# More warming products, new due times for the head, and a new order of the attention steps in a hybrid decoder layer

## The chip, the cores and the metric

One core of one Trainium2 chip runs the whole layer. The metric is the device time of one execution in microseconds (us). Engine names: PE is TensorE (matrix products and transposes), DVE is VectorE, ACT is ScalarE, POOL is GpSimd, SP is SyncE, which here issues the DMAs.

## The reference

A sequence of 512 tokens with width 1024, one layer:

```python
ada = silu(c) @ w_ada + b_ada;  shift, scale, gate = split(ada, 3)
h = rms_norm(x) * (1 + scale) + shift
z = h @ w_in               # 3072 columns: xl | gl | q | k | v | ga, 512 each
y_lru = rg_lru(conv4(xl)) * silu(gl)
q, k = rms_norm per head (8 heads of 64)
y_att = moba_attention(q, k, v) * silu(ga)   # blocks of 256: own block causal, past block whole
out = x + gate * (concat(y_lru, y_att) @ w_out)
```

With 512 tokens there are two blocks, so the attention is ordinary causal attention over tiles of 128 queries.

## The kernel before, in words

All large products are made in three terms (high by high, low by high, high by low parts in float32r), each 512 columns wide. The stages follow one another on PE. In the head, x is loaded in four tiles of 128 tokens (t), its rows are normalised (ACT squares and sums, POOL takes the power, DVE scales, line 423), and eight groups of four transposes (`x_tr(t, i)`: token tile t, half i of the width, line 398) bring it into `xs[i]`, by way of PSUM banks 0, 1, 6 and 7, each used twice. `cb` is silu(c) broadcast to all partitions by two small groups of products (line 380). With it DVE forms two columns of the adaLN product for each slice k of the width (`dot`, line 460); from these come `gs` and the first `h` slices (lines 478 to 492). Then layer 1 (`mm1`, line 509) runs k = 0 to 7 for eight accumulators, `xl0` to `xl3` in banks 4 to 7 and `gl0` to `gl3` in banks 0 to 3. It is followed by k, q and v, the tiles of the attention gate (`g_tile`, line 878), the attention, and the output units (`unit`, line 854).

Warming products (line 442) are 128x128 bf16 products of zeros, two to a group. Their result is read by nobody. The groups have a chain among them, since they write one bank, and they must precede the accumulator that uses their bank next.

Nothing runs in the order of the code. `Plan.schedule` puts all operations in one order by list scheduling with estimated costs: an operation has a due time (`dl`), given or worked back from its successors, and a release time (`rel`). In each turn it takes the engine that can start first, and of that engine's ready operations that could start within 0.35 us of it (0.2 us after the planned time T0 = 14.5) the one with the smallest start plus weighted due time (weight 1.0 before T0, 0.1 after). PE products without a due time of their own take the running sum of PE's costs, so the order of the program is their due order. On the chip each engine runs its own list strictly in this order and waits by semaphores.

The attention is written as steps in `ORDER`: `S` scores of one head pair (hp) for query tiles a and a+1 (a = 2 or 0), then a softmax on DVE, ACT and POOL; `T` transposes of P; `P` the products P.T V; `F` one tile of the attention gate (`F3` in bank 3, else in bank 0); `G` the broadcast of the residual gate, in bank 3; `W` the outputs of the recurrence and the pieces of w_out; `U` the output units of tiles 3 and 2. Joined steps (`P00+P01`) are one visit. The products P.T V of one a and two neighbouring hp share a tile in bank 3:

```python
if hp % 2 == 0:
    pv[a] = bank(f"pv{a}{hp}", 3)
    yy[a] = slot(f"y{a}{hp}")
```

Of the kernel before, what the change touches and what calls it, by code (L numbers as in the profile page):

```python
# [17 lines left out]
P = 128  # L18
S = 512
D = 1024  # L20
# [9 lines left out]

NSLOT = 69
RESERVE = 10
ORDER = ("F3 S22 F S20 S21 T22 G F T21 F3 T20 P20 S23 S01 S02 S00 T00 P21 T23 S03 W T01 P22 T03 T02 P00+P01 "
         "P02 P23 P03 U")
TURN = 0.05
AHEAD = 200.0
SAME, SWITCH = 0.13, 0.2
EPS_PICK, ALPHA = 0.2, 0.1
NDV = 3
DL = dict(cs=60.2, cr=70.1, cbp=18.7, cbc=8.5, rb=47.8, ad=12.3, gs=44.2)  # L40
CBP = 9.0
NSTAGE = 3
NC1 = 1024
T0, TK, LEAD, NWARM, WSTEP, DIP = 14.5, 5.45, 4.0, 36, 0.175, 0.8
RAW, EPS0, ALPHA0, LATER = 4, 0.35, 1.0, 15.5


# [21 lines left out]
class Plan:  # L69
# [13 lines left out]
    def bank(self, name, i):  # L83
        b = Buf(name, "bank", bank=i)
        b.prev = self.banks.get(i)
        self.banks[i] = b
        return b
# [7 lines left out]
    def op(self, fn, costs, reads=(), writes=(), out_lat=None, dl=None, rel=0.0, window=None, sbuf=None, bulk=False, bias=None, mode="full"):  # L95
        o = Op(len(self.ops), fn, costs, out_lat)
        o.mode = mode
        o.bulk, o.bias = bulk, self.bias if bias is None else bias
        o.est, o.sbuf, o.free = rel, True, window
        for lst, wr in ((reads, False), (writes, True)):  # L100
            for x in lst:
                b, key = x if isinstance(x, tuple) else (x, None)
                if b.prev is not None:
                    o.preds.update(b.prev.ops)
                for k2, (ws, rs) in b.state.items():
                    if key is None or k2 is None or key == k2:
                        o.preds.update(ws)
                        if wr:
                            o.preds.update(rs)
                if wr:  # L110
                    if key is None:
                        b.state = {}
                    b.state[key] = ([o], [])
                else:
                    b.state.setdefault(key, ([], []))[1].append(o)
                if not b.ops or b.ops[-1] is not o:
                    b.ops.append(o)
                o.bufs.append(b)
                if b.kind == "bank":
                    o.sbuf = False  # L120
        if sbuf is not None:
            o.sbuf = sbuf
        o.preds.discard(o)
        for p in o.preds:
            p.succs.append(o)
        o.own = "PE" in costs and dl is None
        if "PE" in costs:
            o.dl = o.want = self.pe_t
            self.pe_t += costs["PE"]
        if dl is not None:  # L130
            o.dl = dl
        self.ops.append(o)
        return o
# [111 lines left out]
def hybrid_layer_kernel(ctx: ExitStack, tc, x, small, bgate, wbd, wad, w1, wp, out):  # L245
# [4 lines left out]
    ps = ctx.enter_context(tc.tile_pool(name="ps", bufs=1, space=bass.MemoryType.PSUM))  # L250
    pl = Plan(13.0, 26.0, 40.0, {"DVE": 0.5})
    op, slot, bank, wide = pl.op, pl.slot, pl.bank, pl.wide

    def fixed(name, shape, dt=F32):
        return Buf(name, "fixed", t=cp.tile(shape, dt, name=name))


    def copy(dst, d_ap, src, s_ap, n, psum=False, scale=None, reads=(), bulk=False, bias=None):

        ap = 0 if scale is None else 1  # L260

        def fn(e):
            if e is act:
                act.activation(d_ap(), s_ap(), AF.Copy, scale=1.0 if scale is None else scale())  # L264
            elif scale is None:
                dve.tensor_copy(d_ap(), s_ap())
            else:
                dve.tensor_scalar(d_ap(), s_ap(), scale(), None, op0=MULT)
        return op(fn, {"ACT": c_act(n, ap, psum), "DVE": c_dve(n, ap, psum, not psum)}, [src, *reads], [dst],
                  bulk=bulk, bias=bias)  # L270

    def tt(dst, d_ap, a, a_ap, b, b_ap, n, alu, psum=False, dve_only=False, rel=0.0, window=None):
        def fn(e):
            e.tensor_tensor(d_ap(), a_ap(), b_ap(), op=alu)  # L274
        costs = {"DVE": c_dve(n)} if psum or dve_only else c_tt(n)
        return op(fn, costs, [a, b], [dst], rel=rel, window=window)
# [27 lines left out]
    warm, nhalf = fixed("warm", [P, 128], BF16), fixed("nhalf", [P, 8])  # L304
# [16 lines left out]
    def col(base, i=0, n=1):  # L321
        return sm.t[:, base + i:base + i + n]

    cs, hb, gqk = fixed("cs", [P, 8]), fixed("hb", [P, 8]), fixed("gqk", [P, 1])
    gm, ga_ = fixed("gm", [P, 8, 2]), fixed("gad", [P, 8, 2])
    op(lambda e: act.activation(cs.t, col(C_C, 0, 8), AF.Tanh, scale=0.5), {"ACT": 0.2}, [sm], [cs], dl=DL["cs"])

# [41 lines left out]
    tiny(lambda: dve.tensor_scalar(sp4.t, sp4.t, 4.0, None, op0=MULT), [], [sp4])  # L369


    cr, cb, cbp = fixed("cr", [8, P]), fixed("cb", [P, D]), [bank("cb0", 3), bank("cb1", 5)]
    c8 = sm.t[0:8, C_ROW:C_ROW + P]
    op(lambda e: act.activation(cr.t, c8, AF.Tanh, scale=0.5), {"ACT": 0.22}, [sm], [cr], dl=DL["cr"])
    op(lambda e: dve.scalar_tensor_tensor(cr.t, cr.t, 1.0, c8, op0=ADD, op1=MULT), {"DVE": 0.24}, [sm], [cr], sbuf=False)
    for i in range(2):
        def mm_c(e, i=i):
            for j in range(4):
                d = 4 * i + j
                pe.matmul(cbp[i].t[:, j * P:(j + 1) * P], ident.t[0:8, d:d + 1].to_broadcast([8, P]), cr.t, start=True,  # L380
                          stop=True)
        op(mm_c, {"PE": 0.95}, [cr, ident], [cbp[i]], dl=DL["cbp"] + i)
        v = lambda i=i: cb.t[:, i * 512:(i + 1) * 512]
        copy((cb, i), v, cbp[i], lambda i=i: cbp[i].t, 512, psum=True, bias={})
        pl.ops[-1].dl = DL["cbc"] + i


    xs = [wide(f"xs{i}", 2 + i, (4, S)) for i in range(2)]
    x_bank = [[0, 1, 6, 7], [0, 1, 6, 7]]
    XDL = ((4.2, 2.0, 12.1, 69.3), (18.0, 38.4, 11.1, 38.5))  # L390

    def x_tr(t, i):
        b, w = bank(f"xT{t}{i}", x_bank[i][t]), xw[t // 2]

        def fn(e):
            for k in range(4):
                c0 = (4 * i + k) * P
                pe.transpose(b.t[:, k * P:(k + 1) * P], w.t[:, t % 2, c0:c0 + P], ident.t)  # L398
        op(fn, {"PE": 0.45}, [(w, t), ident], [b], dl=XDL[i][t])
        src = lambda: b.t.rearrange("p (k s) -> p k s", k=4)  # L400
# [9 lines left out]
    for t in range(NT):  # L410
# [9 lines left out]
        if t < RAW:  # L420
# [9 lines left out]
        op(lambda e, dg=dg, rb=rb: pe.matmul(rb.t[:, :P], ones.t, dg.t, start=True, stop=True),  # L430
           {"PE": 0.3}, [ones, dg], [rb], dl=DL["rb"])
        copy(rs[t], lambda t=t: rs[t].t, rb, lambda rb=rb: rb.t[:, :P], P, psum=True, bias={})
# [3 lines left out]


    NA, NB = 512, NC1 - 512
    warm_ps2 = bank("warm2", 2)
    T_ = [T0 + TK * i for i in range(KT)]  # L440
    for i in range(NWARM):
        op(lambda e: [pe.matmul(warm_ps2.t[:, :P], warm.t, warm.t, start=True, stop=True) for _ in range(2)],
           {"PE": 0.2}, [warm], [warm_ps2], dl=40.0, rel=1.0 + WSTEP * i)
    pl.pe_t = 11.0
    acc1 = []
    gs = fixed("gs", [P, 8, 2])
# [482 lines left out]

    for step in ORDER.split():  # L930
        if step[0] == "F":
# [100 lines left out]
```

## Time and profile before

| what | value |
|---|---|
| median of the runs | 235.93 us |
| lowest, highest run | 235.57 us, 325.67 us |
| profiled execution | 235.97 us |
| its span, first to last instruction | 234.1 us |
| PE busy in the span | 226.4 us |
| ACT, DVE, POOL busy | 142.4, 171.2, 55.7 us |

The time of an execution contains 1.9 us around the span of the profile. A view called the timeline lists an engine's instructions in order with the idle time in front of each and what ended it; the windows view gives each engine's busy time in a stretch, and the granted clock of TensorE as a share of 2.4 GHz (1.00 is 2.4, 0.50 is 1.2).

### The profile page before, as it was taken

How to read it: one execution, taken by the hardware profiler on the slowest of the kernel's cores; microseconds unless marked ns; L12 is line 12 of the kernel's file. 1: busy time of each engine (PE TensorE's matmuls, PEld its weight loads, DVE VectorE, ACT ScalarE, POOL GpSimd, SP SyncE). 2: the span in 40 equal slices, each digit the busy share in tenths (PEclk: the TensorE clock that was granted, in tenths of full speed). 3: DMA queues.
4: the chain of work that ended last, by engine and by line, in shares of the span. 5: the costliest groups of instructions: out<-in, count | busy, mean ns of one | idle time of the engine just before them, and what ended most of it. 6: DMA issues, size and time to landing. Idle time of an engine off the chain costs nothing.

```text
span 234.1 us, 3545 instructions
## 1 busy us (share of the span) xinstructions
PE 226.4 (97%) x1244; PEld 185.2 (79%) x1244; DVE 171.2 (73%) x385; ACT 142.4 (61%) x292; POOL 55.7 (24%) x64
## 2 busy tenths in 40 slices
PE   8799999999999999999999999999989999999994
PEld 8677888888887878888888877788768767878893
DVE  0889999997996578898799994669886344665230
ACT  3977787873954999866036425799979851211000
POOL 2400000000040293436502023150937440000001
PEclk9979999999999999999999999999999999999998
DMA  6999999777006205041359340000601114341311
GB/s 214 376 414 412 416 404 415 261 284 279 0 3 245 114 1 179 3 179 34 146 196 392 133 179 4 0 1 0 227 1 45 48 45 166 129 157 58 118 50 48
DMA packets 11447, 37.31 MB, mean 159 GB/s; under 512 B 1186, under 2 KB 2850, under 8 KB 9380
## 3 DMA queue, kind: packets, MB, share of 16 engines
q1 hardware_dynamic: 11428, 37.07, 42.5%
q8 instruction: 10, 0.16, 0.3%
q14 instruction: 9, 0.07, 0.1%
HBM read 34.97 MB, written 2.10 MB: 158 GB/s over the span
## 4 chain that ended last, share of the span: by engine, by line
PE 94%; DMA 2%; DVE 1%; issue 1%; ACT 0%; POOL 0%
PE u L854 19%; PE xl L509 10%; PE k L603 9%; PE g L878 9%; PE v L603 9%; PE q L603 9%; PE gl L509 9%; PE pv L814 4%; PE PT L794 4%; PE S L754 3%; PE xT L398 2%; DMA x<-in_x_dram 2%; PE pr L641 1%; PE cb L380 1%; PE Tk L710 1%
## 5 line engine op out<-in xcount | busy, mean ns | idle before, releaser
L769 ACT ACTIVATE P<-P,st 128x512 f32<-128x512 f32 (+3 forms) x32 | 17.7, 558 | 2.5 <-DVE st L766 2.5
L460 DVE SCALAR_TENSOR_TENSOR st<-st,cb 128x1024 f32<-128x1024 f32 x16 | 18.9, 1216 | 0.0
L778 POOL TENSOR_SCALAR P<-P,st 128x256 f32<-128x256 f32 (+3 forms) x24 | 12.7, 538 | 14.9 <-DVE st L772 12.9
L274 DVE TENSOR_TENSOR o<-u,gbc 128x512 f32<-128x512 f32 (+1 forms) x8 | 5.2, 656 | 14.8 <-PE u L854 14.8
L766 DVE CUSTOM_DVE_ANT_0 P<-S,maskf 128x512 f32<-128x512 f32 (+3 forms) x32 | 13.9, 484 | 2.0 <-PE S L754 2.0
L274 POOL TENSOR_TENSOR xcs0l<-xc,xcs0h 128x512 fp32r<-128x512 f32 x1 | 1.3, 1298 | 52.6 <-ACT xcs0h L264 52.6
L264 ACT ACTIVATE pt<-PT 128x384 f32<-128x384 f32 (+1 forms) x24 | 11.4, 527 | 2.8 <-PE PT L794 2.8
L577 DVE SCALAR_TENSOR_TENSOR ga<-wg,cs,ga 128x512 f32<-128x512 f32 x16 | 12.4, 799 | 0.8 <-DMA wg<-in_wp_dram 0.7
L794 PE MATMUL PT<-ident,P 128*128 128x128 f32 x80 | 11.0, 274 | 0.0
L814 PE MATMUL pv<-pt,vt 128*64 128x256 f32 (+1 forms) x96 | 9.8, 349 | 1.2 <-DVE y L819 1.2
L794 PEld LDWEIGHTS PT<-ident,P 128*128 128x128 f32 x80 | 9.3, 140 | 2.0 <-issue 0.7
L772 DVE RECIPROCAL st<-st 128x1 f32<-128x1 f32 x32 | 4.6, 159 | 8.1 <-ACT P L769 7.8
L814 PEld LDWEIGHTS pv<-pt,vt 128*64 128x64 f32 x96 | 6.4, 136 | 4.4 <-PE S L754 0.8
L274 POOL TENSOR_TENSOR o<-xr,o 128x256 f32<-128x256 f32 x1 | 0.7, 736 | 38.4 <-DVE o L274 38.4
L698 POOL TENSOR_TENSOR msk<-msk,nhalf 128x8 f32<-128x8 f32 x4 | 7.0, 1750 | 8.1 <-DVE msk L696 8.1
L698 POOL TENSOR_TENSOR msq<-msq,nhalf 128x8 f32<-128x8 f32 x4 | 7.0, 1758 | 6.7 <-DVE msq L696 6.7
L475 ACT ACTIVATE gs<-m,gad,gm 128x1 f32<-128x1 f32 x14 | 5.3, 385 | 5.2 <-DVE st L460 5.2
L274 DVE TENSOR_TENSOR w_3l<-wp,w_3h 128x512 fp32r<-128x512 f32 x11 | 8.2, 747 | 0.2 <-ACT w_3h L264 0.2
L264 ACT ACTIVATE qTh<-Tq 128x512 fp32r<-128x512 f32 x4 | 2.4, 597 | 9.4 <-PE Tq L710 9.4
L622 DVE SCALAR_TENSOR_TENSOR xc<-xl,sm,xc 128x511 f32<-128x511 f32 (+2 forms) x12 | 8.0, 740 | 0.0
L398 PE MATMUL xT<-ident,x 128*128 128x128 f32 x32 | 5.9, 338 | 2.0 <-DVE x L423 1.5
L649 ACT ACTIVATE tr<-pr,hb 64x512 f32<-64x512 f32 x8 | 5.4, 681 | 3.5 <-PE pr L641 3.3
(706 smaller groups left out, 773.6 us busy)
## 6 DMA issues: line engine op xcount, KB each, us to landing
wp<-in_wp_dram SPq DMA_DIRECT2D x12, 1024.0 KB, 4.9
st<-in_wad_dram SPq DMA_DIRECT2D x16, 512.0 KB, 7.2
wg<-in_wp_dram SPq DMA_DIRECT2D x4, 1024.0 KB, 4.8
x<-in_x_dram SPq DMA_DIRECT2D x4, 512.0 KB, 5.2
wa<-in_w_dram SPq DMA_DIRECT2D x8, 256.0 KB, 7.6
wb<-in_w_dram SPq DMA_DIRECT2D x8, 256.0 KB, 7.6
xr<-in_x_dram SPq DMA_DIRECT2D x7, 256.0 KB, 3.0
out_dram<-o SPq DMA_DIRECT2D x7, 256.0 KB, 2.0
```

The source lines that it names most:

```text
L264: act.activation(d_ap(), s_ap(), AF.Copy, scale=1.0 if scale is None else scale())
L274: e.tensor_tensor(d_ap(), a_ap(), b_ap(), op=alu)
L460: dve.scalar_tensor_tensor(v, v, 1.0, cb.t, op0=MULT, op1=MULT, accum_out=m.t[:, q:q + 1])
L509: pe.matmul(acc.t, a.t[:, c0:c0 + P], b.t, start=k == 0 and i == 0, stop=k == KT - 1 and i == 2)
L603: pe.matmul(acc.t, hx[kt].t[:, a * P:(a + 1) * P], wx.t, start=s0, stop=s1)
L698: op(lambda e: pool.tensor_tensor(m.t, m.t, nhalf.t, op=ALU.pow), {"POOL": 1.65}, [nhalf], [m])
L766: op(lambda e: dve.tensor_tensor_reduce(p_.t[:, :n], b.t[:, c0:c0 + n], maskf.t[:, 512 - n:], -1.0, -NEG, op0=ADD, op1=ALU.min, accum_out= ...
L769: op(lambda e: act.activation(p_.t[:, :n], p_.t[:, :n], AF.Exp, bias=st.t[:, 0:1], scale=-1.0, accum_out=st.t[:, 1:2]), {"ACT": c_act(n, 2 ...
L794: pe.transpose(b.t[:, o_:o_ + P], p_.t[:, kb * P:(kb + 1) * P], ident.t)
L814: pe.matmul(b.t[64 * e_:64 * e_ + 64, h0 + o_:h0 + o_ + n], vt[kb].t[:, hd * 64:(hd + 1) * 64], pt[e_, kb // 2].t[:, 256 * (kb % 2):256 * ...
L854: pe.matmul(b.t[:, :cn], y_.t[:, c0:c0 + P], w.t[:, cw:cw + cn], start=kt == 0 and i == 0, stop=kt == KT - 1 and i == 2)
L878: pe.matmul(b.t, wx.t[:, c0:c0 + P], hx[kt].t, start=kt == 0 and p == 0, stop=kt == KT - 1 and p == 2)
```

## The change

There are 40 groups of warming products in place of 36, and their release times are spaced by 0.23 us in place of 0.175 us. They write bank 3 in place of bank 2, and the first half of `cb` goes to bank 2 in place of 3. The transposes of x and the operations around `cb` have other due times. The attention steps have another order, and an assertion refuses an order in which an operation touches a tile of a bank that another tile has taken since. `rb`, `ad`, `gs`, `sq` and `wa` in `DL` are read by no line that runs.

```diff
-ORDER = ("F3 S22 F S20 S21 T22 G F T21 F3 T20 P20 S23 S01 S02 S00 T00 P21 T23 S03 W T01 P22 T03 T02 P00+P01 "
-         "P02 P23 P03 U")
+ORDER = ("F3 S21 F F3 F3 T21 S20 T20 G S23 S22 S01 S00 T22 P20 T00 S02 S03 T23 P21 T01 T02 P22+P23 P00 T03 W "
+         "P01 P02 U P03 F")
...
-DL = dict(cs=60.2, cr=70.1, cbp=18.7, cbc=8.5, rb=47.8, ad=12.3, gs=44.2)
+DL = dict(cs=10.0, cr=9.0, cbp=9.0, cbc=13.0, rb=10.9, ad=10.5, gs=12.7, sq=(99, 99, 99, 99), wa=99.0)
...
-T0, TK, LEAD, NWARM, WSTEP, DIP = 14.5, 5.45, 4.0, 36, 0.175, 0.8
+T0, TK, LEAD, NWARM, WSTEP, WDL, DIP = 14.5, 5.45, 4.0, 40, 0.23, 40.0, 0.8
...
+                assert b.kind != "bank" or self.banks[b.bank] is b, b.name
...
-    cr, cb, cbp = fixed("cr", [8, P]), fixed("cb", [P, D]), [bank("cb0", 3), bank("cb1", 5)]
+    cr, cb, cbp = fixed("cr", [8, P]), fixed("cb", [P, D]), [bank("cb0", 2), bank("cb1", 5)]
...
-    XDL = ((4.2, 2.0, 12.1, 69.3), (18.0, 38.4, 11.1, 38.5))
+    XDL = ((7.4, 9.8, 10.6, 8.2), (14.0, 14.1, 14.2, 14.0))
...
-    warm_ps2 = bank("warm2", 2)
+    warm_ps2 = bank("warm2", 3)
     T_ = [T0 + TK * i for i in range(KT)]
     for i in range(NWARM):
         op(lambda e: [pe.matmul(warm_ps2.t[:, :P], warm.t, warm.t, start=True, stop=True) for _ in range(2)],
-           {"PE": 0.2}, [warm], [warm_ps2], dl=40.0, rel=1.0 + WSTEP * i)
+           {"PE": 0.2}, [warm], [warm_ps2], dl=WDL, rel=1.0 + WSTEP * i)
```

## Rows read from the trace of the kernel before

**Rows 1.** The page: the span, and the engines' busy time.
```profile
span 234.1 us, 3545 instructions
PE 226.4 (97%) x1244; PEld 185.2 (79%) x1244; DVE 171.2 (73%) x385; ACT 142.4 (61%) x292; POOL 55.7 (24%) x64
```
**Rows 2.** Timeline of PE, head: start, length, line, operation, count, idle before.
```profile
1.03 5.23 PE L442 MATMUL warm<-warm 128*128 128x128 bf16 x64 [1.03 <-DVE warm L311]
7.78 0.66 PE L398 MATMUL xT<-ident,x 128*128 128x128 f32 x4 [1.52 <-DVE x L423]
8.37 1.15 PE L380 MATMUL cb<-cr,ident 8*128 8x128 f32 x8
...
11.18 2.82 PE L398 MATMUL xT<-ident,x 128*128 128x128 f32 x12
13.79 0.63 PE L442 MATMUL warm<-warm 128*128 128x128 bf16 x4
14.22 1.14 PE L398 MATMUL xT<-ident,x 128*128 128x128 f32 x8
15.20 0.39 PE L442 MATMUL warm<-warm 128*128 128x128 bf16 x4
16.05 0.66 PE L398 MATMUL xT<-ident,x 128*128 128x128 f32 x4 [0.46 <-ACT xs L264]
16.63 1.41 PE L509 MATMUL xl<-h0h,wA0h 128*128 128x512 f32 x4
...
18.80 1.07 PE L509 MATMUL xl<-h0h,wA0l 128*128 128x512 f32 x4
...
22.67 0.39 PE L509 MATMUL xl<-h1h,wA1h 128*128 128x512 f32 x1
```
**Rows 3.** Windows: busy time of PE, PEld, DVE, ACT, POOL; clock; DMA share; GB/s.
```profile
5.00:6.00 1.00, 1.00 (x22) 1.00 (x20) 0.00 (x0) 0.97 (x3) 0.00 (x0) 1.00 0.82 256
...
10.50:11.00 0.50, 0.50 (x7) 0.50 (x5) 0.50 (x1) 0.50 (x2) 0.23 (x1) 1.00 0.99 406
11.00:11.50 0.50, 0.50 (x4) 0.32 (x3) 0.43 (x4) 0.39 (x2) 0.50 (x1) 0.51 1.02 401
...
14.00:14.50 0.50, 0.50 (x7) 0.50 (x5) 0.50 (x1) 0.46 (x1) 0.00 (x0) 0.58 1.02 410
```
**Rows 4.** Timeline of DVE in the head: last tile of x, gs, first and second h.
```profile
11.56 0.75 DVE L423 TENSOR_SCALAR x<-x,r 128x1024 f32<-128x1024 f32 x1
...
14.83 0.16 DVE L479 TENSOR_TENSOR gs<-gs,gad 128x2 f32<-128x2 f32 x1
16.03 0.55 DVE L492 TENSOR_SCALAR h0h<-xs,gs 128x512 fp32r<-128x512 f32 x1 [1.04 <-ACT xs L264]
...
21.19 0.54 DVE L492 TENSOR_SCALAR h1h<-xs,gs 128x512 fp32r<-128x512 f32 x1
```
**Rows 5.** Timeline of PE in the attention: a visit of S, two of P.T V.
```profile
146.07 0.50 PE L754 MATMUL S<-kTh,qTh 64*128 64x512 f32 x2
...
172.89 1.73 PE L814 MATMUL pv<-pt,vt 128*64 128x256 f32 x16 [0.72 <-DVE y L819]
...
187.97 1.52 PE L814 MATMUL pv<-pt,vt 128*64 128x256 f32 x16 [0.53 <-DVE y L819]
```
**Rows 6.** Windows in the attention, columns as in rows 3.
```profile
145.00:150.00 5.00, 5.00 (x35) 3.87 (x34) 2.98 (x10) 2.83 (x6) 0.85 (x2) 1.00 0.00 0
...
155.00:160.00 5.00, 5.00 (x31) 4.27 (x30) 3.92 (x9) 5.00 (x14) 2.50 (x4) 1.00 0.00 0
...
185.00:190.00 5.00, 4.47 (x44) 3.17 (x43) 2.17 (x6) 2.54 (x5) 3.19 (x3) 1.00 0.01 5
```
**Rows 7.** The page: exponentials and copies of transposed P on ACT.
```profile
L769 ACT ACTIVATE P<-P,st 128x512 f32<-128x512 f32 (+3 forms) x32 | 17.7, 558 | 2.5 <-DVE st L766 2.5
...
L264 ACT ACTIVATE pt<-PT 128x384 f32<-128x384 f32 (+1 forms) x24 | 11.4, 527 | 2.8 <-PE PT L794 2.8
```
**Rows 8.** The chain that ended last: a unit's part that needs no attention.
```profile
176.51 2.94 PE u L854 x12
```

## The prediction

> **What bounds the kernel.** I read the page first: PE is busy for 226.4 of 234.1 us [rows 1], so there are 7.7 us without work on PE, and nothing but PE's own work can be worth more. Then PE's timeline, for where these 7.7 us lie: 1.03 before the first product, 1.52 before the first transposes, 0.46 before the last ones [rows 2], 0.72 and 0.53 in the attention, each behind DVE's reading of an earlier P.T V [rows 5]. The remaining 3.4 us are the tail behind the last product, which the change doesn't touch. From 16.05 us on PE has no other gap than the two in the attention. So the time is the moment when the first real product starts (16.63 us [rows 2]), plus PE's work, plus the attention's gaps.
>
> Third, the clock: it is at 2.4 GHz until 11.0 us, at 1.2 GHz until 14.4 us, and then at 2.4 GHz [rows 3]. Before it falls PE was idle from 6.26 to 7.78 us, and then did 8 transposes and 16 products for `cb`. In the slow stretch 12 transposes took 2.82 us, 0.235 each; eight at the end of it and after took 1.14 us, 0.143 each [rows 2]. The slow stretch so costs 12 x 0.09 = 1.1 us for the transposes, and with the four warming products and the end of `cb` in it some 1.3 us.
>
> Fourth, DVE's timeline: what is the earliest start of the first product if PE weren't late? `gs` is there at 14.99 us, but `h0h` starts only at 16.03, because the last tile of `xs[0]` came late, though its x was scaled at 12.31 us [rows 4]. Without that, `h0h` would be done at 14.99 + 0.55 = 15.54 us, and the first product would start at about 15.6: at most 1.0 us earlier. The chain of DVE behind `gs` sets that end.
>
> **The change, part by part.** *Warming products.* Before, 64 of the 72 products run before the first transposes, and 8 after it [rows 2]. The planner puts one group of two in each 0.2 us, so 32 groups fill its time until 1.0 + 32 x 0.2 = 7.4. Spaced by 0.23, only 28 groups are released by then. The other 12 groups, 24 products, then stand in PE's list behind the first transposes: 16 more than before. Where? Between 8.37 and 11.18 us the list holds `cb` and transposes with due times of 7.4 to 10.6. A group's due time is worked back from the accumulator that follows it (gl3, about 16.1, less 0.2 for each group still to come), so the 29th has about 13.7. These groups give way to the first transposes of each tile and to `cb`, and compete with the second ones (14.0 to 14.2). Most fill the idle time that the planner sees at 14.4 to 15.8, in front of the first product; on the chip PE has no idle time there but 0.46 us. PE takes its list in order, so they delay it. The price of one: four take 0.43 us from start to start at 13.79, at the low clock, and 0.39 us for four at 15.20 [rows 2], so 0.10; the lower bound is 0.045, from 22 in the window from 5 to 6 us [rows 3]. 16 x 0.045 = 0.7, 16 x 0.10 = 1.6. I take 1.1, between them, as some run back to back and some between transposes.
>
> *Due times of the transposes.* All four of `xs[0]` now come before those of `xs[1]`. No work is saved. But the gap of 0.46 us goes, because a bank's copy (ACT, 0.6 us) now has other work in front of the next user. And the first four products of layer 1, which take 1.41 us where the four at 18.80 take 1.07 [rows 2], lose a wait for the last copy: 0.34. Together -0.8 us. What is late next: `h0h` at 15.0, which leaves 1.0 us, so the limit isn't reached. Behind it DVE has `h1h` done at 21.73 for a product at 22.67 [rows 2, 4]; it moves with `h0h`, so its 0.94 us of cover stay.
>
> *Due times of `cs`, `cr`, `cbp`, `cbc`; banks 2 and 3.* The order by due time and readiness is still first transposes, `cb`, second transposes, `cb`. I cost them at nothing; if `cb` came one group of transposes later, the two dots behind it and the first product would come 0.6 us later. The swap of banks moves the wait for the warming products from gl2 to gl3, one product later.
>
> *The clock.* The 56 products in front of the first transposes end some 0.5 us sooner, so PE is idle for about 2.0 us in place of 1.5, and then does the same work as before until 11.2. I see nothing that removes the fall; it may come earlier. I take no change in its cost, with -1.3 (it goes) and +1.3 (it lasts twice as long) as bounds. The trace shows the fall after 8 transposes and 16 small products, and the rise after 12 transposes with 4 warming products among them [rows 2, 3]. The Trainium skill (TensorE: Matmul & The Clock Gate, Part 4) says that transposes don't count as a busy PE for the clock; by that the warming products alone would hold it, and with more of them behind the first transposes the sum would get the -1.3. The rise at 14.4 with hardly any of them speaks against so strict a reading.
>
> Head: +1.1 - 0.8 + 0 = +0.3 us.
>
> *Order of the attention.* There are 8 visits of S, 8 of T and 7 of P before and after, so the work on PE and its switches stay. `P23` came after `P00+P01`, both in bank 3, and waited 0.53 us for DVE's reading [rows 5]; `P22+P23` joined don't. -0.5. The 0.72 us in front of `P22` came from DVE, which still had to read `P20` and `P21`; now `T01` and `T02` lie between, four groups of transposes as cover. I take half of it, -0.35, as DVE's queue of weight splits may still hold the reading up. Against this the gate's tiles are gathered: three of the four `F` come in a row, two in bank 3, so that the second must wait for ACT and DVE to empty it. `S20` (1.4 us of PE) stands ready to fill that. But `G` too needs bank 3 twice, and `S22` needs the banks of `S23`, four reductions on DVE. I take +0.3 for such gaps, with 0 and +1.8 as bounds (the second rival). `W` behind `T03` and `U` before `P03` change creation order alone; the pieces of w_out and the x tiles on SP's queue keep their due times from the output units, and the last `F` takes a unit that would come next anyway.
>
> Attention: -0.5 - 0.35 + 0.3 = -0.55, taken as -0.6.
>
> Sum against the profiled execution of 235.97 us (span 234.1 and 1.9 around it): +0.3 - 0.6 = -0.3, so 235.7. The median of the runs is 235.93, the same for this purpose.
>
> **The rivals.** *The clock holds, or the slow stretch becomes harmless.* If a few of the 24 late products land between 8 and 11 us and the clock stays at 2.4 GHz, the slow stretch's 1.3 us go. DVE's chain allows 1.0 of it at most, and the late products can follow the first real ones. 235.97 - 1.0 - 0.6 = 234.4; with both attention gaps gone, 1.25, it is 233.7. For it: `rel` reaches 10.0. Against it: the due times above.
>
> *The softmax starves PE* (slower). Before, the S visits stand between tiles of the gate (one starts at 146.07), and ACT has 2.2 of 5 us free at 145 to 150, is full from 155 to 160, and has 2.5 free at 185 to 190 [rows 5, 6]. Now `S20` is due after three gate tiles, and `S23` and `S22` after all four. One visit for a = 2 costs ACT four exponentials (0.6 to 0.7 each, 2.7) and four copies at 0.5 (2.0) [rows 7], 4.7 us. If one visit's share is pushed out of the free time before 155 and PE runs dry, the cover is a unit's part of 2.94 us that needs no attention [rows 8], so 4.7 - 2.9 = +1.8. It decides from the point at which the unfinished softmax is longer than PE's other ready work. 235.97 + 0.3 + 1.8 - 0.5 = 237.6. For it: full ACT. Against it: PE's other transposes and two more units in banks 4 and 5, once S is done.
>
> *The slow stretch starts earlier and lasts* (slower). With 2.0 us idle in front of the transposes the clock falls before 8 us and comes back as late as before: 8 more transposes at +0.09, 16 `cb` products that are at most doubled (+1.1 at most), and the late warming products at 0.10, 1.6 in place of 1.1. +0.7 + 0.6 + 0.5 = +1.8, with the attention's -0.6: 237.5.
>
> *The change doesn't do what it says*: the longer release may put nothing into the stretch that it seems made for. That is in my forecast.
>
> **How the numbers follow.** Forecast 235.7 (half of the chance, 235.0 to 236.4 from the warming price of 0.7 to 1.6 and the attention's gaps); clock holds, 0.2; softmax starves PE, 0.17; slow stretch longer, 0.13. The range reaches into the three: 234.0 to 237.6. A measurement of this kernel tells apart some 2 per cent, 4.7 us. Faster by that would need all idle time and the whole slow stretch to go, which the DVE chain excludes: 0.01. Slower needs both slower rivals at once and more: 0.04. Within: 0.95.
>
> **What would show it.** Right: 56 warming products in front of the first transposes and 24 after; the first real product at 16.5 to 17.2 us; the clock still at 1.2 GHz for some 3.4 us before 15; no wait for y in front of `P22+P23`. Wrong: the granted clock at 1.00 throughout the head and the first product below 16; or gaps on PE between 158 and 185 behind ACT or DVE that add up to more than 1.5 us; or a stall in layer 1 behind `h1`, which would mean that DVE isn't covered.

## The result and the profile after

The median of 22 runs is 233.69 us, against 235.5 us for 22 runs of the kernel before on the same chips. The ratio of the runs compared is 0.9942, with a 95% interval of 0.9915 to 0.9969: faster by 0.6%, some 1.4 us. Runs more than 1.5% above the fastest of the same kernel are left out of all such ratios, and with them some of the long clock losses of the table below. The profiled execution took 232.88 us.

The page of the changed kernel: span and busy time.
```profile
span 231.1 us, 3569 instructions
...
PE 225.1 (97%) x1252; PEld 184.3 (80%) x1252; DVE 173.5 (75%) x385; ACT 141.5 (61%) x292; POOL 59.7 (26%) x64
```
PE is busy for 1.3 us less than in [rows 1], though it does eight products more, and it is idle for 6.0 us in place of 7.7. What PE waits for, in the changed kernel's list of waits on PE (line waited for: total, times, longest):
```profile
PE warm L443 <- DVE warm L312: 1.0, 1, 1.0
PE xT L399 <- DVE x L424: 0.8, 1, 0.8
PE xl L510 <- ACT wB0h L265: 0.5, 1, 0.5
```
All three lie in the head. The two gaps of the attention [rows 5] are gone and none has come in their place. The head on PE's timeline of the changed kernel, to be laid beside [rows 2]:
```profile
1.03 5.31 PE L443 MATMUL warm<-warm 128*128 128x128 bf16 x58 [1.03 <-DVE warm L312]
7.18 0.66 PE L399 MATMUL xT<-ident,x 128*128 128x128 f32 x4 [0.84 <-DVE x L424]
...
11.14 0.39 PE L443 MATMUL warm<-warm 128*128 128x128 bf16 x4
11.52 2.66 PE L399 MATMUL xT<-ident,x 128*128 128x128 f32 x20
14.02 1.06 PE L443 MATMUL warm<-warm 128*128 128x128 bf16 x16
15.61 1.17 PE L510 MATMUL xl<-h0h,wA0h 128*128 128x512 f32 x4 [0.53 <-ACT wB0h L265]
...
17.30 0.28 PE L443 MATMUL warm<-warm 128*128 128x128 bf16 x2
...
21.67 0.39 PE L510 MATMUL xl<-h1h,wA1h 128*128 128x512 f32 x1
```
58 products stand in front of the first transposes and 22 behind. The first real product starts at 15.61 us, 1.02 earlier than before. The first transposes start 0.6 us earlier (7.18 in place of 7.78), because the first tile of x landed earlier in this execution, but that isn't where the 1.02 comes from: DVE scales the last tile of x only 0.18 us earlier (11.38 in place of 11.56), and the other 0.9 is the wait of 1.04 us in front of `h0h` in [rows 4], which is gone. It belongs to the lost clock and not to the old head: in e_order below, with the old head and a kept clock, `h0h` doesn't wait. The clock in the changed kernel, windows as in [rows 3], and DVE, as in [rows 4]:
```profile
2.00:2.50 0.50, 0.50 (x7) 0.50 (x6) 0.00 (x0) 0.00 (x1) 0.20 (x1) 1.00 0.54 188
...
5.50:6.00 0.50, 0.50 (x13) 0.50 (x10) 0.13 (x2) 0.50 (x2) 0.36 (x1) 1.00 0.38 157
...
10.50:11.00 0.50, 0.44 (x4) 0.35 (x4) 0.47 (x4) 0.50 (x3) 0.39 (x1) 1.00 1.01 418
11.00:11.50 0.50, 0.50 (x7) 0.34 (x5) 0.50 (x2) 0.50 (x3) 0.17 (x1) 1.00 0.98 381
...
14.00:14.50 0.50, 0.50 (x11) 0.49 (x10) 0.50 (x4) 0.50 (x2) 0.00 (x0) 1.00 1.11 442
```
```profile
11.38 0.74 DVE L424 TENSOR_SCALAR x<-x,r 128x1024 f32<-128x1024 f32 x1
...
14.65 0.16 DVE L480 TENSOR_TENSOR gs<-gs,gad 128x2 f32<-128x2 f32 x1
14.92 0.55 DVE L493 TENSOR_SCALAR h0h<-xs,gs 128x512 fp32r<-128x512 f32 x1
```
No fall of the clock is recorded before the tail. The 1.00 at 2.0 us is no reading, though: the column reads 1.00 until the first recorded rise, which came at 5.04 us here and at 4.18 in the kernel before. Up to it PE gets 7 to 8 warming products into half a microsecond, behind it 13. So where the prediction says that the clock is at 2.4 GHz until 11.0 us, it holds from 4.2 us on only.

The first product starts as soon as `h0h` is done (14.92 + 0.55 = 15.47 us). The list of waits names ACT's `wB0h`, which ended within 0.03 us of it, but the product doesn't need it: in the run e_oldwarm below it started at 15.40 us, and `wB0h` ended at 15.56. So DVE's chain bounds the start here, at the moment that the prediction's fourth view gave as the earliest. In all seven profiles in which the clock was kept, whatever their head, `h0h` starts 3.53 to 3.54 us after DVE began to scale the last tile of x (here 11.38 and 14.92); in the kernel before it was 4.47.

Behind the head the two kernels run alike until the gate's tiles (116.8 and 116.9 us from the first real product). From there, the chain of the changed kernel that ended last:
```profile
132.69 6.80 PE g L879 x30
139.49 1.43 PE S L755 x12
140.92 9.75 PE g L879 x42
...
165.44 3.18 PE pv L815 x32
...
181.27 3.18 PE pv L815 x32
...
190.38 37.31 PE u L855 x186
```
In the kernel before, the same chain goes from 133.61 us (first gate tile) to 230.68 (194.49 and 36.19 us of units). That is 97.07 us; here it is 132.69 to 227.69, 95.00 us. Two thirds of what the two profiles differ by (231.1 against 234.1) lie here.

### The profile page after: what moved, and what is told of

The parts are those of the page before. It is cut to its first block, busy times and chain, and to the rows that moved or that the text cites. A ratio compares the mean times of both kernels' runs of the same rounds, so it can differ in the third digit from the quotient of the medians.

```text
span 231.1 us, 3569 instructions
## 1 busy us (share of the span) xinstructions
PE 225.1 (97%) x1252; PEld 184.3 (80%) x1252; DVE 173.5 (75%) x385; ACT 141.5 (61%) x292; POOL 59.7 (26%) x64
## 4 chain that ended last, share of the span: by engine, by line
PE 93%; DMA 2%; ACT 2%; SPq 1%; DVE 1%; issue 0%; POOL 0%
PE u L855 19%; PE k L604 10%; PE g L879 10%; PE xl L510 10%; PE gl L510 10%; PE q L604 10%; PE v L604 9%; PE PT L795 4%; PE pv L815 4%; PE S L755 4%; DMA x<-in_x_dram 2%; PE pr L642 1%; PE xT L399 1%; PE Tk L711 1%; PE Tq L711 1%; ACT xs L265 1%
## 5 line engine op out<-in xcount | busy, mean ns | idle before, releaser
L779 POOL TENSOR_SCALAR P<-P,st 128x256 f32<-128x256 f32 (+3 forms) x19 | 11.2, 595 | 10.4 <-DVE st L773 9.5
L578 DVE SCALAR_TENSOR_TENSOR ga<-wg,cs,ga 128x512 f32<-128x512 f32 x16 | 11.4, 764 | 0.8 <-DMA wg<-in_wp_dram 0.8
L275 POOL TENSOR_TENSOR w_1l<-wp,w_1h 128x512 fp32r<-128x512 f32 x6 | 8.7, 1443 | 13.1 <-ACT w_1h L265 13.1
L275 DVE TENSOR_TENSOR w_3l<-wp,w_3h 128x512 fp32r<-128x512 f32 x12 | 8.8, 736 | 0.0
L275 DVE TENSOR_TENSOR w_0l<-wp,w_0h 128x512 fp32r<-128x512 f32 x10 | 8.0, 796 | 0.3 <-ACT w_0h L265 0.3
L443 PE MATMUL warm<-warm 128*128 128x128 bf16 x80 | 7.0, 263 | 1.0 <-DVE warm L312 1.0
```

## The experiments

Each execution also gave its mean granted clock over the span. It falls into three groups: 0.995 or more (kept: no fall of the clock recorded in the head), 0.989 to 0.994 (a short loss), and 0.986 or less (a long one). The table counts the executions and has the median of each group. The kernel before ran beside each of the three groups of experiments, with medians of 235.27, 235.26 and 235.22 us. "In front" is the number of warming products ahead of the first transposes or of `cb`, whichever comes first.

| kernel | in front | kept: n, us | short: n, us | long: n, us |
|---|---|---|---|---|
| before (beside the experiments) | 64 | 45, 234.65 | 33, 235.67 | 5, 238.62 |
| changed | 58 | 9, 232.85 | 5, 233.73 | 8, 235.55 |
| e_head | 58 | 7, 234.69 | 3, 235.50 | 2, 236.85 |
| e_order | 64 | 4, 232.87 | 4, 234.12 | 0 |
| e_oldwarm | 64 | 7, 232.73 | 3, 233.64 | 2, 238.31 |
| e_olddue | 58 | 3, 233.41 | 3, 234.99 | 6, 237.20 |
| e_d1 | 58 | 7, 233.96 | 1, 234.37 | 4, 236.28 |
| e_w48 | 48 | 0 | 0 | 12, 236.09 |
| e_w68 | 68 | 3, 233.30 | 3, 233.65 | 0 |
| e_o68 | 68 | 9, 232.99 | 3, 234.41 | 0 |
| e_w76 | 76 | 4, 234.16 | 7, 234.03 | 1, 234.96 |

The run e_nowarm, with two warming products, isn't in the table: its 12 executions read 0.997 to 1.000, since no fall is recorded, but in its profile the first rise came only at 18.94 us. The mean tells nothing of the clock ahead of the first rise.

**Head alone (e_head).** The changed kernel with the old order of the attention, without the assertion.
```diff
-ORDER = ("F3 S21 F F3 F3 T21 S20 T20 G S23 S22 S01 S00 T22 P20 T00 S02 S03 T23 P21 T01 T02 P22+P23 P00 T03 W "
-         "P01 P02 U P03 F")
+ORDER = ("F3 S22 F S20 S21 T22 G F T21 F3 T20 P20 S23 S01 S02 S00 T00 P21 T23 S03 W T01 P22 T03 T02 P00+P01 "
+         "P02 P23 P03 U")
```


> New head (warming products, due times, banks), old order of the attention steps. Theory A (two parts that add up: the head gives about 1.0 us by an earlier first product, the attention about 2.0 us by its missing gaps): the first product at about 15.6 us, the two gaps of 0.72 and 0.53 us in the attention still there, 1.0 us below the kernel before, and the gain varies from run to run with the clock in the head. Theory B (the gain is the clock alone): the whole gain, 2 to 3 us where the clock stays at 2.4 GHz. Theory C (the attention alone): no difference.

Measured: ratio 0.9998 (0.9974 to 1.0022), no difference, as theory C says. The first product came at 15.45 us as in theory A, without the gain that A ties to it. The two gaps are there, as one line of its waits shows:
```profile
PE pv L814 <- DVE y L819: 1.2, 2, 0.7
```
**Order alone (e_order).** The opposite edit, in the kernel before.
```diff
-ORDER = ("F3 S22 F S20 S21 T22 G F T21 F3 T20 P20 S23 S01 S02 S00 T00 P21 T23 S03 W T01 P22 T03 T02 P00+P01 "
-         "P02 P23 P03 U")
+ORDER = ("F3 S21 F F3 F3 T21 S20 T20 G S23 S22 S01 S00 T22 P20 T00 S02 S03 T23 P21 T01 T02 P22+P23 P00 T03 W "
+         "P01 P02 U P03 F")
```

> Old head, new order of the attention steps. Theory A: the first product at 16.0 to 16.6 us, no gap on PE in the attention, 1.5 to 2.0 us below the kernel before. Theory B: the same as before within 0.4 us. Theory C: the whole gain.

Measured: ratio 0.9927 (0.9902 to 0.9953), some 1.7 us: the whole gain. Theory C holds. What theory A says of this run came out too (first product at 16.16 us, no gap in the attention, 1.7 us); it fails over the head, by e_head. From the first start of a gate tile to the start of the last product of the kernel, the timelines give 96.95 us before, 96.71 in e_head, and 94.87 both here and in the changed kernel: 2.08 us less. And the head: with the old due times and a kept clock, the first product waits for `h0h` as well. From e_order's timeline of PE:
```profile
7.60 0.66 PE L398 MATMUL xT<-ident,x 128*128 128x128 f32 x4 [0.41 <-DVE x L423]
...
16.16 1.20 PE L509 MATMUL xl<-h0h,wA0h 128*128 128x512 f32 x4 [0.37 <-DVE h0h L492]
```
**Old warming products (e_oldwarm).**
```diff
-T0, TK, LEAD, NWARM, WSTEP, WDL, DIP = 14.5, 5.45, 4.0, 40, 0.23, 40.0, 0.8
+T0, TK, LEAD, NWARM, WSTEP, WDL, DIP = 14.5, 5.45, 4.0, 36, 0.175, 40.0, 0.8
```


> The changed kernel with the old 36 groups of warming products, spaced by 0.175 us; due times, banks and order as changed. If the later warming products hold the clock, the granted clock falls below 2.4 GHz in more of the runs here, and the time is 0.5 to 1.5 us above the changed kernel. If they only lie in front of the first real product, the time is 0 to 0.8 us below it, and the clock falls as often in both.

Measured: ratio 0.9919 (0.9894 to 0.9944). With a kept clock it is 0.1 us below the changed kernel, so the later products cost next to nothing. PE's timeline shows why: the time that they take is there as a wait when they aren't (the second line is ACT's).
```profile
15.40 1.16 PE L510 MATMUL xl<-h0h,wA0h 128*128 128x512 f32 x4 [0.91 <-DVE h0h L493]
...
14.89 0.67 ACT L265 ACTIVATE wB0h<-wb 128x512 fp32r<-128x512 f32 x1
```
The clock didn't fall in more of the runs: 5 of 12, against 13 of 22, too few to tell apart. So nothing shows that the later products hold the clock.

**Old due times (e_olddue).** All else as changed.
```diff
-DL = dict(cs=10.0, cr=9.0, cbp=9.0, cbc=13.0, rb=10.9, ad=10.5, gs=12.7, sq=(99, 99, 99, 99), wa=99.0)
+DL = dict(cs=60.2, cr=70.1, cbp=18.7, cbc=8.5, rb=47.8, ad=12.3, gs=44.2)
...
-    XDL = ((7.4, 9.8, 10.6, 8.2), (14.0, 14.1, 14.2, 14.0))
+    XDL = ((4.2, 2.0, 12.1, 69.3), (18.0, 38.4, 11.1, 38.5))
```

> The changed kernel with the old due times of the transposes and of cs, cr, cb; the warming products, banks and order as changed. If the due times give what the head gains, the first product comes at 16.4 us or later, since the last tile's transposes stand behind others and behind warming products: 0.8 us or more above the changed kernel. If the warming products give it, the difference is under 0.3 us.

Measured: ratio 0.9979 (0.9946 to 1.0012), the median 235.52 us. In its profiled execution the first product came at 19.22 us, with the clock lost from 9.4 to 16.3 us. But this mixes two things: 0.6 us with a kept clock (233.41 against 232.85, but three executions only, from 232.94 to 233.52), and a long loss in half of the runs. So it doesn't settle what due times do alone; e_o68 does.

**How many warming products in front: 76, 48, 2.** A new theory (D) came from the runs up to here: a long loss is frequent where 58 products stand in front (16 of 46 executions) and rare with 64 (2 of 51); in the whole table it is 20 of 58 and 7 of 103. Fewer products in front also end earlier, so the count and the idle time behind them go together in all these runs. These kernels have 32 groups and no product behind the first transposes; the planner then sets `cb` first.
```diff
-T0, TK, LEAD, NWARM, WSTEP, WDL, DIP = 14.5, 5.45, 4.0, 40, 0.23, 40.0, 0.8
+T0, TK, LEAD, NWARM, WSTEP, WDL, DIP = 14.5, 5.45, 4.0, 32, 0.175, 40.0, 0.8
...
-        op(lambda e: [pe.matmul(warm_ps2.t[:, :P], warm.t, warm.t, start=True, stop=True) for _ in range(2)],
+        op(lambda e, i=i: [pe.matmul(warm_ps2.t[:, :P], warm.t, warm.t, start=True, stop=True) for _ in range(3 if i >= 20 else 2)],
```
(48: `range(2 if i < 16 else 1)`; two products: `NWARM` 1 with the changed line's two.)

> The changed kernel with 76 warming products, all in front of the first transposes and none behind them (32 groups spaced by 0.175 us, the last 12 of three products). Theory D (the clock is lost for longer when fewer warming products stand in front of the first transposes): no run with a granted clock of 0.985 or less over the span, most at 0.995 or more, median at or below 233.0 us. Theory E (the new due times make the longer loss): such runs in about a third of the cases, as with the changed kernel.

> The same with 48 warming products, all in front of the first transposes, none behind. Theory D: half of the runs or more at a granted clock of 0.985 or less, these 2 us or more above those that keep the clock; median 234.5 us or more. Theory E: as with 76 products.

> The changed kernel with two warming products in all. Theory D: the clock is low in every run for the whole head, the first real product at 17.5 us or later, median 236 us or more. If warming doesn't matter: within 0.5 us of the changed kernel.

Measured: 48 in front, long losses in 12 of 12, ratio 1.0030 (1.0000 to 1.0061). 76 in front, 1 of 12, but ratio 0.9968 (0.9944 to 0.9992): with a kept clock it is 1.3 us slower than the changed kernel. Theory D's other signs for it failed: the median is 234.16 us and not 233.0, one loss is long, and 4 of 12 kept the clock, not most. With two products: 236.33 us, ratio 1.0047 (1.0021 to 1.0074). That is 3.5 us above the changed kernel with a kept clock, but 2.2 above e_w76 (234.16), which has the same order of `cb` and the transposes, so warming by itself is worth about 2 us here. Theory E falls: the due times are the same in all three. PE's timeline of e_w48, with the idle time in which the clock fell:
```profile
1.03 4.27 PE L443 MATMUL warm<-warm 128*128 128x128 bf16 x48 [1.03 <-DVE warm L312]
7.89 2.04 PE L381 MATMUL cb<-cr,ident 8*128 8x128 f32 x8 [2.59 <-DVE gqk L343]
...
13.76 5.02 PE L399 MATMUL xT<-ident,x 128*128 128x128 f32 x24
18.70 1.55 PE L510 MATMUL xl<-h0h,wA0h 128*128 128x512 f32 x4
```
24 transposes take 5.02 us there, 0.21 each, where 20 took 2.66 in the changed kernel, 0.13 each. And of e_w76:
```profile
8.21 1.12 PE L381 MATMUL cb<-cr,ident 8*128 8x128 f32 x8
...
14.76 0.66 PE L399 MATMUL xT<-ident,x 128*128 128x128 f32 x4 [0.83 <-ACT xs L265]
16.64 1.72 PE L510 MATMUL xl<-h0h,wA0h 128*128 128x512 f32 x4 [1.22 <-DVE h0h L493]
```
Here the first half of `cb` starts 0.4 us later than in the changed kernel and the second 0.85 (10.29 against 9.44), with eight transposes between them in place of four. PE then waits twice, and `h0h` starts at 16.05 us, 1.13 later: 0.55 of it is there at DVE's scaling of the last tile of x (11.93 against 11.38), and the rest is the copy of the last transposes, which DVE did at 15.45. This execution had a short loss, from 17.1 to 20.5 us, so the profile doesn't show what the 1.3 us with a kept clock are.

**The pair divided again (e_d1).** The changed kernel without the assertion, and:
```diff
-ORDER = ("F3 S21 F F3 F3 T21 S20 T20 G S23 S22 S01 S00 T22 P20 T00 S02 S03 T23 P21 T01 T02 P22+P23 P00 T03 W "
-         "P01 P02 U P03 F")
+ORDER = ("F3 S21 F F3 F3 T21 S20 T20 G S23 S22 S01 S00 T22 P20 T00 S02 S03 T23 P21 T01 T02 P22 P00+P01 T03 W "
+         "P02 P23 U P03 F")
```


> The changed kernel in which the pair P22 and P23 is divided again by P00, P01 and P02, in the new order (P22 P00+P01 T03 W P02 P23 U P03). Theory F (the divided pair costs its wait in bank 3): a wait on PE for DVE's reading in front of P23 comes back, 0.4 to 0.8 us, and the time from the first gate tile to the last product is 95.3 to 95.8 us in place of 94.87. Rival (the wait was due to DVE being late with other work at that moment): no wait, no difference above 0.2 us.

Measured: ratio 0.9981 (0.9950 to 1.0012); with a kept clock 233.96 us, 1.1 above the changed kernel. From the first gate tile to the last product it is 95.80 us, 0.93 more. Theory F holds at the upper end; the wait in front of `P23`, from its timeline of PE:
```profile
184.16 1.52 PE L814 MATMUL pv<-pt,vt 128*64 128x256 f32 x16 [0.71 <-DVE y L819]
```
**68 in front (e_w68, e_o68).** 36 groups spaced by 0.175 us, four of them with a third product; the first with all else as changed, the second with the old due times and banks and the new order:
```diff
-for _ in range(2)],
+for _ in range(3 if 28 <= i < 32 else 2)],
```

> The changed kernel with the old 36 groups of warming products spaced by 0.175 us, four of which (the last in front of the first transposes) have three products: 68 in front, 8 behind. Theory D (products in front of the first transposes hold the clock, those behind only lie in the way): no run with a granted clock of 0.985 or less, and those at 0.995 or more as fast as the changed kernel's (232.6 to 233.1 us), median 232.9 to 233.3 us, better than both kernels. Theory E (the new due times make the longer loss): such runs in 2 to 4 of 12.

> The kernel before with the new order of the attention steps and 68 warming products in front of the first transposes, 8 behind; old due times. If the due times are worth nothing as long as the chain of VectorE sets the first product: the same as the run beside it with the new due times, within 0.4 us in the median. If the new due times give 0.5 us or more: 233.6 us or more.

Measured: ratios 0.9928 (0.9903 to 0.9953) and 0.9932 (0.9909 to 0.9954). No long loss in 18 executions, as theory D said. But e_w68's six executions have a median of 233.53 us, above what was expected. The cause stays open: in its profile the first transposes start 0.06 us after x is scaled, as in e_oldwarm, so the four more products didn't hold them up there. With the old due times the first product comes as early as with the new ones. From e_o68's timeline of PE:
```profile
15.44 1.19 PE L509 MATMUL xl<-h0h,wA0h 128*128 128x512 f32 x4 [0.29 <-DVE h0h L492]
```
The two medians, 233.17 and 233.53 us, lie within the 0.4 us expected. So the due times are worth nothing here. All kernels with the new order and 64 or 68 products in front have ratios of 0.9919 to 0.9932, below the changed kernel's 0.9942, but the intervals overlap: none is shown to beat it.

## Why the prediction was right, and where its terms were off

The forecast was 235.7 us, 0.3 below the profiled execution, within 234.0 to 237.6 and within 2%. The sign held. The range held by the ratio (0.9942 of 235.93 is 234.6 us); the median itself, 233.69 us, lies 0.3 below it. Of a gain of 1.4 us by ratio the forecast had 0.3, both terms of the sum were mis-sized, and only the width of the range covers that.

By the prediction's own signs the order came out right (no wait for `y` in front of `P22+P23`) and the head wrong: in the profiled execution no fall of the clock is recorded, and the first product came at 15.61 us, below 16. The number of the first rival, 233.7 us, is the one that was measured, but not for its reason. It has the late products hold the clock, and e_oldwarm, with fewer of them, kept it no less often (7 of 12, against 9 of 22).

*Order of the attention: -0.6 forecast, -2.08 measured.* The waits were right in their place. The 0.53 us in front of `P23` went; dividing the pair again brought 0.71 back. Of the 0.72 us in front of `P22` I took half, since DVE's queue could hold the reading up; all of it went. In the chain, 12.7 us of other work lie between the end of one pair of `P` and the start of the next (168.62 to 181.27), not only `T01` and `T02`. The +0.3 for new gaps was 0: `S20` (151.43 in the chain) filled the change of bank between two gate tiles as expected. The step that failed is "the work on PE and its switches stay". I counted visits in `ORDER` and not how often a gate tile is interrupted. Summed from start to start over the timelines before and after, gate tiles went from 22.49 to 22.10 us, in 3 stretches in place of 7; S from 9.90 to 8.78 (0.72 of it the wait behind it); P.T V from 10.01 to 9.26 (0.53 of it the wait); transposes of P and `gb` rose by 0.21 together. Of S another 0.36 is a wait that PE's list doesn't name, as another product was running. Two products of the visit at 174.56, before, and the same two in the changed kernel:
```profile
175.30 0.68 PE L754 MATMUL S<-kTh,qTh 64*128 64x256 f32 x2
...
173.20 0.33 PE L755 MATMUL S<-kTh,qTh 64*128 64x256 f32 x2
```
Before, the second of the two started 0.30 us behind the first, at 175.60, by its semaphore behind DVE, which read scores of an earlier visit until 175.54. So of 2.08 us, 1.6 are waits, and the other 0.5 is shorter stretches on PE, 0.39 of it in the gate tiles. That this is the price of switching was not tried by itself, and over all kinds the stretches are 36 in place of 39.

*Warming products: +1.1 forecast, about +0.1 measured.* The count was near (58 and 22 against 56 and 24). The price failed, because it was charged against PE's list while the first product waits for `h0h` anyway. I had found that bound (15.6 us), but used it only as a limit for gains. With a kept clock the first product starts at 15.4 to 16.2 us in every kernel that sets the first transposes first, with either warming schedule and either set of due times, and it moves with DVE's scaling of the last tile of x (11.18 to 12.01 us). *Due times: -0.8 forecast, 0 measured*, for the same reason. The gap of 0.46 us that I booked as a gain is there with the old due times and a kept clock too (0.46 in e_order, 0.47 in e_o68) and costs nothing, as the first product waits for `h0h` behind it. The first four products take 1.16 to 1.20 us in all seven profiles with a kept clock, whatever the due times, so their 1.41 belonged to an execution in which the clock had been lost.

*The clock: 0 forecast.* This is the part that I had least right. I read the fall at 11.0 us as the kernel's habit. It was lost in 38 of 83 executions of the kernel before and kept in the others, so the profile before was one draw of two, worth 1.0 us (short losses 235.67 against 234.65). The change does what the third rival said in part of the runs: fewer products in front and a loss that lasts (8 of 22, some 2.7 us above a kept clock and 1.8 above a short loss; the rival's +1.8 counts from an execution with a short loss). That such a loss starts earlier is seen in e_olddue alone, with the same 58 in front (9.4 us). That takes back some of the attention's gain: 0.9942 against 0.9927 for the order alone, a difference within the intervals. Head: +0.3 forecast, 0 by e_head with an interval of half a microsecond either way.

*The softmax starves PE: refuted.* The rows of the changed kernel beside [rows 6]:
```profile
145.00:150.00 5.00, 5.00 (x23) 4.14 (x23) 4.38 (x7) 3.45 (x8) 1.54 (x2) 1.00 0.00 0
155.00:160.00 5.00, 5.00 (x29) 4.06 (x29) 4.19 (x9) 4.53 (x12) 2.77 (x3) 1.00 0.20 46
...
185.00:190.00 5.00, 5.00 (x45) 3.41 (x44) 4.57 (x10) 4.12 (x9) 1.46 (x1) 1.00 0.28 95
```
Some of ACT's work did move later, to 185 to 190 us (4.12 in place of 2.54), but PE is busy for all 5.00 of 5 us in each, with units as cover.

*Transposes and the clock.* The prediction doubted, for the rise at 14.4 us, that transposes don't count; the runs bear the doubt out (last section).

## What to carry to other kernels

Before an edit is priced on an in-order engine's list, ask what the instruction behind it waits for: work in front of a wait is free up to the wait's length, and a gap removed there gains nothing. One profile is one draw of the clock: look at the granted clock of several executions before a slow stretch is booked as something that a change could remove, or leave. A clock column that reads 1.00 ahead of its first change may be no reading: count the products in a window. When a list is reordered, count not only the steps but how often a long stretch of one kind is broken, and look for waits that hide behind a running product.

## What was not expected of the hardware

The same kernel kept or lost TensorE's clock in the head from one execution to the next (45 and 38 of 83). The first rise varies too: in the eleven profiles with 48 products or more it came at 4.0 to 6.8 us, though PE had done the same until then, warming products from 1.03 us on. Whether the one goes with the other no run here shows. In the kernels with 48 products and two, the clock came back after nothing but transposes. In e_w48 PE did nothing but transposes from 13.76 us until the first real product at 18.70, and the granted clock rose before it, at 17.69:
```profile
10.00:11.00 1.00, 1.00 (x6) 1.00 (x7) 1.00 (x2) 0.97 (x3) 0.39 (x1) 0.50 1.01 412
17.00:18.00 1.00, 1.00 (x7) 0.82 (x5) 0.83 (x3) 0.53 (x1) 0.00 (x0) 0.66 1.06 426
18.00:19.00 1.00, 0.94 (x6) 0.72 (x6) 0.90 (x2) 0.97 (x3) 0.00 (x0) 1.00 0.97 379
```
In e_nowarm the last 24 transposes ran from 13.88 us, 0.22 us each, and the rise that the trace records at 18.94 came just ahead of the first real product:
```profile
13.88 5.33 PE L399 MATMUL xT<-ident,x 128*128 128x128 f32 x24
18.98 0.96 PE L510 MATMUL xl<-h0h,wA0h 128*128 128x512 f32 x3
```
The Trainium skill (TensorE: Matmul & The Clock Gate, Part 4) says that transposes don't count as a busy PE for the clock; this measurement differs from it, for transposes of 128x128 in float32, and it decides here.
